# Turned attention tiles issued from SP, and a head norm with VectorE transposes, in a streaming-encoder layer

## The chip, the core and the metric

The kernel runs on one core of a Trainium2 chip. A core has TensorE (PE: matmuls, with PEld for the loading of its weights), VectorE (DVE), ScalarE (ACT), GpSimd (POOL) and SyncE (SP, which issues transfers); every engine works through its own list of instructions in order, and the engines wait for each other by semaphores. DMAs are issued from the queues of SP, ACT and POOL. The metric is the device time of one execution in microseconds (us).

## The reference

One layer of a streaming encoder, float32, sequence 512, model width 1024. A normed input goes through one input projection into four token mixers, whose outputs are each projected to 1024 channels, multiplied by a gate made of the same normed input, added up, and projected once more. Cross-attention into 256 memory tokens and a gated MLP follow. The change touches the mixers A and F and the preparation of the memory tokens:

```
# A: differential attention, 4 heads, two score maps each, chunk-causal mask
p = softmax(where(mask, s, -inf));  a = p[:, :, 0] - lam * p[:, :, 1]
o = einsum('bhqk,bkhe->bqhe', a, v)          # then a norm over each head's 128 channels
# F: forgetting attention, 8 heads, causal mask
s = q.k * scale + c[q] - c[k];  p = softmax(where(mask, s, -inf));  o = p.v
# norm of a head:  o * rsqrt(mean(o*o over 128 channels) + EPS) * gain
```

## The kernel before, in words

Products are made in three passes of float32r: every operand x is held as hi (x rounded by ScalarE, a copy) and lo (x minus hi, by VectorE), and each product is hi·hi, hi·lo, lo·hi into one PSUM bank of 512 columns. So each block of weights is loaded by SP into `wr` (L176, two buffers), cast by ACT into `wh` (L192) and its rest taken by DVE into `wl` (L193), four buffers each. A matmul helper (L235) and a PE transpose helper (L241) make nearly all of PE's work.

PSUM has eight banks in four pairs: `ps_mm` (projections), `ps_av` (in the attention stages the attention outputs; outside of them it alternates with `ps_mm`), `ps_sc` (scores), `ps_tr` (transposes).

The order of work. `run_blocks` goes through a list of weight blocks (the projections) and after each calls `bg.tick()`: a background planner that keeps a clock of estimated TensorE time (`bg.clock`, raised by each matmul and transpose), earns credit at 0.7 of it, and steps the background generators while they have credit. Each `yield cost, wait` of a generator tells what it has spent and how long it wants to stay away. The attention heads are such generators: `a_task(h)` for heads 0 to 3 of A, `f_task(p)` for pairs 0 to 3 of F. The framework's scheduler then fixes the order on every engine; `tc.issue_after(x)` keeps an instruction behind x there. `evacuations` holds the last ACT instruction that emptied a PSUM bank of a projection or a gate, `last_weights` the last weight cast.

One step of a head makes 128 rows of scores (`scores`, into `ps_sc`), adds mask or bias and takes the maximum (DVE, L929 in A, L1123 in F), exponentiates on ACT (L934, L1129), and scales by the reciprocal sum: in A by ACT (L938) and DVE (L939), in F for the pair's head j=1 by DVE (L1134) and for j=0 by ACT (L1136). In F POOL makes the bias `fbias` (L1117, L1119) from `ck`, the running sum of the log gates, which is spread over the partitions by a DMA from `crows`.

The values' product needs the probabilities transposed. Near heads (A's head 3, F's pairs 2 and 3) use PE transposes. Far heads (A's 0 to 2, F's 0 and 1) turn squares of 32x32 on DVE (L848), write the tile to DRAM (`put`, L853, queue of ACT) and read it back turned (`get`, L861, queue of POOL in A, of ACT in F), and split it in place (`split_in_place`: ACT cast L867, DVE rest L868). At the end of an A head its output is copied from `ps_av` (ACT, L948), transposed by four PE transposes, squared (ACT L954), summed (DVE L956), raised to -1/2 on POOL (`rstd_of`, L277 and L280), multiplied (DVE L958), transposed back by four PE transposes and split into `y8b` (ACT L158, DVE L159).

Mixers C and D come first, to about 208 us of the span; A's heads run beside projections and the gates of branch C to about 345; then come the values and forget gates of F (`vf_jobs`, `forget_gates`), F's pairs beside the gates and branch of A to about 535; then the gate of F's branch, during which `mem_task` turns the memory tokens (put on ACT, get on POOL, L1305), then cross-attention and MLP.

## Time and profile before

| what | value |
|---|---|
| median of 3 runs | 1052.34 us (1051.72 to 1052.66) |
| profiled execution, its own time | 1052.56 us |
| its span | 1050.8 us |
| PE busy | 1039.2 us, 99% of the span |
| DVE busy | 807.2 us, 77% |
| ACT busy | 508.9 us, 48% |
| POOL busy | 157.7 us, 15% |
| granted TensorE clock | 0.998 |

The span runs from the first to the last instruction of the profiled execution; its own time has 1.8 us more around it. Busy shares are means over stages. PE's matmuls overlap in the records, so the pace of PE is read from the starts of neighbouring matmuls and not from the duration of one: the record of a 512-column matmul says 0.39 us, but the next one starts 0.23 us later.

### The profile page before, as it was taken

To read this page: it belongs to the slowest core of one execution; us is meant where nothing else is said; L and a number is where in the kernel's file an instruction comes from. 1 tells how busy PE (TensorE), PEld (TensorE's weight loads), DVE (VectorE), ACT (ScalarE), POOL (GpSimd) and SP (SyncE) were. 2 spreads that over 40 slices of the span, in tenths; PEclk is the share of its full clock that TensorE was granted. 3 is DMA by queue.
4 is the path that set the end of the run, shared out by engine and by line. 5 is a ranking of instruction groups with operands and counts; after the bars stand their busy time and mean duration, and the time that the engine had idled before them with its cause. 6 is when DMAs were issued, how large, how long until landed. Compare 5 with 4: busy or idle time off the path is not lost.

```text
span 1050.8 us, 14439 instructions
## 1 busy us (share of the span) xinstructions
PE 1039.2 (99%) x5255; PEld 883.0 (84%) x5255; DVE 807.2 (77%) x1265; ACT 508.9 (48%) x838; POOL 157.7 (15%) x253
## 2 busy tenths in 40 slices
PE   9999999999999999999999999999999999999997
PEld 8888888888888988788888899999888888888886
DVE  7899998687777458776577898776767777667796
ACT  5322222376566355665434665655343333445662
POOL 4001000101210114422111031121112111111001
PEclk9999999999999999999999999999999999999999
DMA  7954333324433245652346834235676666725672
GB/s 249 316 164 104 103 99 100 101 83 124 134 104 111 60 120 172 182 149 82 100 154 230 277 121 124 78 101 182 194 246 221 220 223 219 220 81 181 214 216 80
DMA packets 175708, 163.85 MB, mean 156 GB/s; under 512 B 12543, under 2 KB 146924, under 8 KB 175637
## 3 DMA queue, kind: packets, MB, share of 16 engines
q1 hardware_dynamic: 152995, 119.91, 38.0%
q10 hardware_dynamic: 19122, 31.47, 8.9%
q0 software_dynamic: 3520, 11.56, 3.7%
q8 instruction: 41, 0.67, 0.3%
q14 instruction: 30, 0.25, 0.1%
HBM read 139.43 MB, written 23.48 MB: 155 GB/s over the span
## 4 chain that ended last, share of the span: by engine, by line
PE 90%; issue 4%; DVE 2%; ACT 1%; DMA 1%; POOL 1%; ACTq 0%; POOLq 0%; DVEq 0%
PE ps_mm L235 47%; PE ps_av L235 29%; PE ps_sc L235 7%; PE ps_tr L235 4%; PE ps_tr L241 2%; DMA ptl<-turned 1%; PE ps_mm L453 1%; PE ps_av L453 1%; POOL fbias L1117 0%; DMA xs<-in_x 0%; DVE qk L808 0%; ACT wh L192 0%; ACTq L861 0%; DVE e L1123 0%; DVE wl L193 0%
## 5 line engine op out<-in xcount | busy, mean ns | idle before, releaser
L192 ACT CAST wh<-wr 128x1024 fp32r<-128x1024 f32 (+1 forms) x140 | 146.7, 1048 | 258.9 <-PE ps_mm L235 156.9
L193 DVE TENSOR_TENSOR wl<-wr,wh 128x1024 fp32r<-128x1024 f32 (+1 forms) x140 | 174.2, 1245 | 86.3 <-ACT wh L192 86.0
L235 PE MATMUL ps_mm<-hth,wh 128*128 128x512 f32 (+1 forms) x616 | 230.8, 381 | 1.0 <-ACT wh L192 0.7
L235 PE MATMUL ps_mm<-hth,wl 128*128 128x512 f32 (+1 forms) x616 | 229.9, 379 | 0.0
L235 PE MATMUL ps_mm<-htl,wh 128*128 128x512 f32 (+1 forms) x616 | 229.8, 379 | 0.0
L235 PEld LDWEIGHTS ps_mm<-hth,wh 128*128 128x128 f32 x616 | 114.2, 188 | 22.5 <-ACT wh L192 1.1
L235 PEld LDWEIGHTS ps_mm<-hth,wl 128*128 128x128 f32 x616 | 114.0, 188 | 21.5
L235 PEld LDWEIGHTS ps_mm<-htl,wh 128*128 128x128 f32 x616 | 114.1, 188 | 20.4
L235 PE MATMUL ps_av<-htl,wh 128*128 128x512 f32 (+1 forms) x328 | 122.6, 374 | 0.0
L235 PE MATMUL ps_av<-hth,wh 128*128 128x512 f32 (+1 forms) x328 | 122.5, 373 | 0.0
L235 PE MATMUL ps_av<-hth,wl 128*128 128x512 f32 (+1 forms) x328 | 122.4, 373 | 0.0
L688 DVE SCALAR_TENSOR_TENSOR y<-y,par,y 128x508 f32<-128x508 f32 (+29 forms) x120 | 82.5, 726 | 0.1
L235 PEld LDWEIGHTS ps_av<-hth,wl 128*128 128x128 f32 x328 | 61.7, 188 | 10.9
L235 PEld LDWEIGHTS ps_av<-hth,wh 128*128 128x128 f32 x328 | 61.6, 188 | 10.9
L235 PEld LDWEIGHTS ps_av<-htl,wh 128*128 128x128 f32 x328 | 61.6, 188 | 10.8
L1683 DVE TENSOR_TENSOR wl<-dw,wh 128x1024 fp32r<-128x1024 f32 x32 | 40.0, 1256 | 15.5 <-ACT wh L1682 15.3
L1682 ACT CAST wh<-dw 128x1024 fp32r<-128x1024 f32 x32 | 33.4, 1051 | 22.6 <-PE ps_tr L235 8.1
L1117 POOL TENSOR_SCALAR fbias<-ck,cq 128x128 f32<-128x128 f32 (+3 forms) x32 | 28.3, 887 | 71.9 <-DVE st L1123 66.5
L1630 ACT ACTIVATE th<-c 128x512 f32<-128x512 f32 x22 | 13.9, 632 | 48.3 <-DVE c L615 48.3
L615 DVE SCALAR_TENSOR_TENSOR c<-ps_mm,par,c 128x510 f32<-128x510 f32 (+1 forms) x44 | 32.7, 744 | 0.7
L235 PE MATMUL ps_mm<-y8b,wh 128*128 128x512 f32 x96 | 30.6, 396 | 0.3 <-ACT ge L1165 0.3
L615 DVE SCALAR_TENSOR_TENSOR c<-ps_av,par,c 128x510 f32<-128x510 f32 (+1 forms) x40 | 29.8, 745 | 0.6
(486 smaller groups left out, 2103.5 us busy)
## 6 DMA issues: line engine op xcount, KB each, us to landing
wr<-in_w_up SPq DMA_DIRECT2D x44, 512.0 KB
wr<-in_w_in SPq DMA_DIRECT2D x38, 512.0 KB
wr<-in_w_gate SPq DMA_DIRECT2D x32, 512.0 KB
wp<-in_w_down ACTq DMA_DIRECT2D x22, 512.0 KB
sums<-wp ACTq DMA_DIRECT2D x22, 512.0 KB
dw<-sums SPq DMA_DIRECT2D x44, 256.0 KB
wr<-in_w_branch SPq DMA_DIRECT2D x16, 512.0 KB
wide<-in_w_out SPq DMA_DIRECT2D x12, 512.0 KB
```

The costliest lines, as they stand in the source:

```text
L192: last_weights[:] = [order(A.copy(hi, raw[:, :n])).ins, low.tensor_tensor(lo, raw[:, :n], hi.bitcast(F32), ALU.subtract).ins]
L193: low.tensor_tensor(lo, raw[:, :n], hi.bitcast(F32), ALU.subtract).ins]
L235: steps_of[:] = [PE.matmul(ps, lhs, rhs, start=start, stop=stop).ins]
L241: turns.append(PE.transpose(ps, x, ident[:n, :n]).ins)
L453: keep(PE.matmul(banks[c][:, :S // 2], w[p == 1][:, k, c * P:(c + 1) * P], ht[p == 2][:, i * 4 + k, :S // 2], start=(i, p, k) == (0, 0, 0) ...
L615: ins = V.scalar_tensor_tensor(dst[:, s:], src[:, :S - s], w(k), dst[:, s:], ALU.mult, ALU.add)
L688: ins = V.scalar_tensor_tensor(dst[:, s:], src[:, :S - s], pc("conv_dw", k * 4 + j), dst[:, s:], ALU.mult, ALU.add)
L1117: G.tensor_scalar(bias[:, :w], ck[j][:, :w], -1.0, cq[:, qt, head:head + 1], ALU.mult, ALU.add)
L1630: A.activation(th, c[:, 0], AF.Silu)
L1682: A.copy(hi, x)
L1683: V.tensor_tensor(lo, x, hi.bitcast(F32), ALU.subtract)
```

## The change

Four things are changed together.

- Transfers of turned tiles: `put` and `get` of the far heads, and both transfers of `mem_task`, are issued by SP. `get` isn't kept behind `evacuations` any more.
- The in-place split of A's far heads puts its ACT cast behind the last weight cast (`last_weights`) instead of the last evacuation.
- In F's far pairs the scaling of j=0 is done by DVE like that of j=1.
- The norm of A's heads: the output tile is turned by DVE in squares of 32x32 within SBUF, squared by ACT from SBUF, summed over the 32 columns of each square row (128x16), completed over the four partition groups by `over_channels` (one PE matmul of 16 columns into a `ps_tr` bank, L872), EPS is added by DVE, POOL raises 128x16 values to -1/2, DVE multiplies and turns back, and the split reads SBUF. The eight PE transposes of each head and one of its two `ps_tr` banks go.

```diff
     def put(e, w):
...
-        A.dma_start(d, e[:, :, :w])
+        SP.dma_start(d, e[:, :, :w])
         return d
...
-    def get(d, n, pt, local, queue=A):
-        with tc.issue_after(evacuations[0]) if queue is A else ExitStack():
-            queue.dma_start(part_of(pt[1], n, local).bitcast(F32), d.rearrange("(a j) (b x) -> (j b) a x", j=32, b=4))
-
-    def split_in_place(n, pt, local):
+    def get(d, n, pt, local):
+        SP.dma_start(part_of(pt[1], n, local).bitcast(F32), d.rearrange("(a j) (b x) -> (j b) a x", j=32, b=4))
+
+    def split_in_place(n, pt, local, after=evacuations):
         hi, lo = (part_of(x, n, local) for x in pt)
         raw = lo.bitcast(F32)
-        with tc.issue_after(evacuations[0]):
+        with tc.issue_after(after[0]):
             A.copy(hi, raw)
         V.tensor_tensor(lo, raw, hi.bitcast(F32), ALU.subtract)
...
-                    split_in_place(qt + 1, pt, qt % 2)
+                    split_in_place(qt + 1, pt, qt % 2, last_weights)
...
-                    get(es.pop(qt)[:, 0], qt + 1, pt, qt % 2, G)
+                    get(es.pop(qt)[:, 0], qt + 1, pt, qt % 2)
...
+        V.transpose(e[:, 1], e[:, 0])
+        A.activation(e[:, 0], e[:, 1], AF.Square, scale=1.0 / math.sqrt(P))
+        ms = m1p.tile([P, S // 32], F32, tag="ms4", name="ms4")
+        V.tensor_reduce(ms, by_token(e[:, 0]), AX.X, ALU.add)
+        yield 2.0, 4.0
         ps = bank("tr")
-        for t in range(NT):
-            transpose(ps[:, t * P:(t + 1) * P], e[:, 0, t * P:(t + 1) * P])
-        A.activation(e[:, 1], ps, AF.Square, scale=1.0 / math.sqrt(P))
-        ms = m1p.tile([P, NT], F32, tag="ms4", name="ms4", bufs=2)
-        V.tensor_reduce(ms, e[:, 1].rearrange("p (t c) -> p t c", t=NT), AX.X, ALU.add)
-        r = rstd_of(m1p, [ms], NT)
-        V.tensor_tensor(e[:, 0].rearrange("p (t c) -> p t c", t=NT),
-                        ps.rearrange("p (t c) -> p t c", t=NT),
-                        r.unsqueeze(2).to_broadcast([P, NT, P]), ALU.mult)
-        yield 1.5, 3.5
-        ps2 = bank("tr")
-        for t in range(NT):
-            transpose(ps2[:, t * P:(t + 1) * P], e[:, 0, t * P:(t + 1) * P])
+        over_channels(ps[:, :S // 32], ms)
+        V.tensor_scalar(ms, ps[:, :S // 32], EPS, None, ALU.add)
+        G.tensor_tensor(ms, ms, nhalf[:, :1].to_broadcast([P, S // 32]), ALU.pow)
+        yield 0.2, 4.0
+        V.tensor_tensor(by_token(e[:, 1]), by_token(e[:, 1]), ms.unsqueeze(2).to_broadcast([P, S // 32, 32]), ALU.mult)
+        V.transpose(e[:, 0], e[:, 1])
         if "a" not in y:
             y["a"] = (y8b(), y8b())
-        split(ps2, y["a"][0][:, h], y["a"][1][:, h], half["dn"])
-        yield 0.6, 0.0
+        split(e[:, 0], y["a"][0][:, h], y["a"][1][:, h], half["dn"])
+        yield 2.4, 0.0
...
-                    if j:
+                    if j or far:
                         V.tensor_scalar(e[:, j, :w], e[:, j, :w], st[:, 6 + j:7 + j], None, ALU.mult)
...
-            A.dma_start(d.rearrange("(p x) -> p x", p=P), m_t)
-            G.dma_start(y_t.rearrange("p (a x) -> p a x", a=4), d.rearrange("(a j b x) -> (j b) a x", a=4, j=32, b=4))
+            SP.dma_start(d.rearrange("(p x) -> p x", p=P), m_t)
+            SP.dma_start(y_t.rearrange("p (a x) -> p a x", a=4), d.rearrange("(a j b x) -> (j b) a x", a=4, j=32, b=4))
```

The changed estimates of cost in the `yield` lines shift where the planner places the heads' steps, so the order of matmuls on PE differs from the A stage to the end of the F stage. On PE 32 transposes of 128 columns go and 4 matmuls of 16 columns come; SP gets 52 transfers that ACT (20 puts, 16 gets, 2 of the memory) and POOL (12 gets, 2 of the memory) issued.

## Prediction

> **What bounds the kernel now.** I read the page's head first, then the waits of each engine between 200 and 535 us (the stages that the change reaches), then the timeline around each wait of PE.

> ```profile
> span 1050.8 us, 14439 instructions
> PE 1039.2 (99%) x5255; PEld 883.0 (84%) x5255; DVE 807.2 (77%) x1265; ACT 508.9 (48%) x838; POOL 157.7 (15%) x253
> PE ps_sc L235 <- DVE st L1123: 0.8, 1, 0.8
> PE ps_mm L235 <- ACT wh L192: 0.7, 1, 0.7
> PE ps_mm L235 <- ACT ge L1165: 0.3, 1, 0.3
> PE ps_mm L235 <- DVE qk L808: 0.2, 1, 0.2
> PE ps_tr L241 <- ACT e L948: 0.2, 1, 0.2
> 208.00:345.00 137.00, 136.77 (x682) 115.79 (x681) 103.38 (x230) 84.27 (x168) 16.79 (x26) 1.00 0.39 114
> 430.00:535.00 105.00, 104.28 (x528) 88.22 (x529) 69.28 (x145) 57.30 (x118) 26.88 (x41) 1.00 0.39 113
> ```

> PE is the bound, in the touched stages too (136.77 of 137 us; the columns are the stretch, its length and the busy us of PE, PEld, DVE, ACT and POOL). All idle time of PE between 200 and 535 us is in five waits. So a change here counts in two ways: by the matmuls that PE no longer has to issue, and by the few places where PE waits. Work of DVE, ACT, POOL and the queues costs nothing until it makes such a place.

> **PE's own work: -2.9 us.**

> ```profile
> 345.14 1.03 PE L241 MATMUL ps_tr<-ident,e 128*128 128x128 f32 x8
> 345.93 0.36 PE L235 MATMUL ps_mm<-wl,hth 128*128 128x256 f32 x1
> 346.13 0.28 PE L235 MATMUL ps_mm<-wh,htl 128*128 128x256 f32 x1
> 346.25 0.29 PE L235 MATMUL ps_mm<-wh,hth 128*128 128x256 f32 x1
> 186.10 0.29 PE L872 MATMUL ps_tr<-bn,across 128*128 128x16 f32 x2
> 186.24 0.48 PE L235 MATMUL ps_mm<-y8b,wh 128*128 128x512 f32 x1
> 186.55 0.39 PE L235 MATMUL ps_mm<-y8b,wl 128*128 128x512 f32 x1
> 186.78 0.62 PE L235 MATMUL ps_mm<-y8b,wh 128*128 128x512 f32 x2
> ```

> Eight transposes start at 345.14 and the next matmul at 345.93: 0.099 us each. The matmul behind them takes 0.20 to the next start where the one after takes 0.12: 0.08 lost per run of transposes. Thirty-two of them in up to eight runs cost 3.16 to 3.8 us; I take 3.5. A matmul with 16 columns (two records) takes 0.14, and the matmul behind it 0.31 in place of 0.23, so four cost 0.56 to 0.88; I take 0.6. Net -2.9 (bounds -2.3 and -3.2).

> **Waits that go: -3.0 us.**

> ```profile
> 427.56 0.62 PE L235 MATMUL ps_sc<-qk 128*128 128x512 f32 x2
> 429.03 0.73 PE L235 MATMUL ps_sc<-qk 128*128 128x512 f32 x2 [0.85 <-DVE st L1123]
> 430.42 0.47 PE L235 MATMUL ps_mm<-hth,wh 128*128 128x512 f32 x1 [0.66 <-ACT wh L192]
> 427.36 1.17 DVE L848 STREAM_TRANSPOSE e<-e 128x256 f32<-128x256 f32 x2 [0.90 <-DMA turned<-e]
> 437.82 2.35 ACTq L861 DMA_DIRECT2D ptl<-turned  x4
> 440.22 0.72 ACT L1136 ACTIVATE e<-e,st 128x512 f32<-128x512 f32 x1 [2.98 <-issue]
> 440.72 0.56 PE L235 MATMUL ps_sc<-qk 128*128 128x128 f32 x4
> 441.57 0.73 PE L235 MATMUL ps_mm<-y8b,wh 128*128 128x512 f32 x2 [0.30 <-ACT ge L1165]
> 350.11 0.62 PE L241 MATMUL ps_tr<-ident,e 128*128 128x128 f32 x4
> 350.94 0.66 PE L241 MATMUL ps_tr<-ident,e 128*128 128x128 f32 x4 [0.22 <-ACT e L948]
> ```

> By starts: two 512-column scores need 0.46, so 427.56 to 429.03 lost 1.0 and 429.03 to 430.42 lost 0.9. DVE came late there because its turn (L848) waited for a put that ACT had issued, with the scores' eviction (L1123) queued behind it. Four 128-column scores need 0.4, so 440.72 to 441.57 lost 0.4; ACT had first issued four gets (2.35 us), and the gate's Tanh (L1165) stood behind the delayed scaling. With put and get on SP neither queue holds compute, and one of the two scalings leaves ACT. 350.11 to 350.94 lost 0.4 in a transpose that is removed. With 0.2 to 0.3 at another place that the new order loosens, 3.0 go; the wait for L808 near 220 us, ahead of all edits, stays. Bounds: nothing goes but the 0.4 of the removed transpose, or all 3.0.

> **Waits that come: +3.6 us.** They follow from the new order of instructions, with durations from these rows:

> ```profile
> L818 DVE TENSOR_TENSOR qk<-ps_mm,qk 64x512 fp32r<-64x512 f32 x16 | 11.0, 688 | 3.5 <-ACT qk L816 3.4
> L929 DVE CUSTOM_DVE_ANT_0 e<-ps_sc,mask_a 128x384 f32<-128x384 f32 x8 | 4.2, 549 | 0.3 <-PE ps_sc L235 0.2
> L948 ACT COPY e<-ps_av 128x512 f32<-128x512 f32 x4 | 2.3, 581 | 3.5 <-PE ps_av L235 3.4
> L868 DVE TENSOR_TENSOR ptl<-ptl,pth 128x256 fp32r<-128x256 f32 x7 | 2.9, 423 | 1.2 <-ACT pth L867 1.2
> ACT pth L867 <- DMA ptl<-turned: 12.5, 7, 4.5
> ```

> - Near 264 us a projection block wants the `ps_mm` bank which two L818 subtractions empty, and these now stand behind a score eviction (L929) that PE itself feeds 1.25 us of matmuls earlier: 0.55 + 2 x 0.69 - 1.25, about 0.7, and 0.1 for the read of the maximum. 0.8 (0 to 1.4, both subtractions).
> - At the ends of heads 2 and 3 (about 344 and 348 us) the copy L948 out of `ps_av` is followed, in place of four transposes, by matmuls of `vf_jobs` into that bank: 0.44 us of other work before the first, none before the second. The row above with 0.44 us of cover lost 0.4; without cover it is 0.8. Sum 1.2 (0.4 to 1.6).
> - Head 2's last gets are issued when the value product of the first half has freed `ptl`, 6 us of matmuls ahead of use, and must land and be cast in that time. ACT's seven waits for such a tile were 1.8 us in the mean (the L867 row); I take 0.2, since most of one is covered (0 to 1.8).
> - The F stage begins with scores whose bias waits for the chain of forget gates; in the new order fewer matmuls lie beside it. What PE wants behind them is again a bank that two subtractions of 0.69 empty: 0.5 (0 to 1.4).
> - Near 404 us a gate product on DVE (L1177) stands behind in-place splits of F's pair 0, and these wait for gets: two or three L868 between, 0.9 (0 to 1.7, four).

> **Work that stays hidden.**

> ```profile
> L727 DVE STREAM_TRANSPOSE xn<-y 128x512 f32<-128x512 f32 x4 | 2.7, 697 | 0.0
> L722 POOL TENSOR_TENSOR bn<-bn,nhalf 128x16 f32<-128x16 f32 x1 | 2.9, 2930 | 96.2 <-DVE bn L705 96.2
> L1134 DVE TENSOR_SCALAR e<-e,st 128x512 f32<-128x512 f32 x4 | 1.9, 487 | 0.1
> SPq L176 <- DVE wl L193: 202.4, 33, 21.5
> ```

> A head's norm puts two square transposes (1.4 us) and a small addition more on DVE, about 1.5 us, and the power on POOL, 128x16 like the row of L722, takes 2.9. Nothing on PE waits for it but the 16-column matmul, which the planner places a step later, and `y8b` is needed only by the branch in the F stage. The far scaling puts eight operations on DVE, of 0.49 at the largest width: under 3.9 us over some 60. DVE idles 33 and 36 us in the two stretches shown, so both lie beside PE as long as they don't stand ahead of an eviction; where they do is in the list above. POOL loses 12 gets, whose waits for their puts stood ahead of its memsets and biases, ACT 16 gets and 20 puts. SP takes them: it waits 202 us of these 335 for a free `wr`, because the weights are loaded far ahead, so a weight load behind a get that waits for its put is late against nothing at once. If that cover is gone, each costs PE what the put takes. In the memory stage (from 535 us) two transfers move in the same way: nothing.

> **The sum.** -2.9 - 3.0 + 3.6 = -2.3 against the profiled execution's 1052.56, so 1050.3; that run lies 0.2 above the median of the three, so 1050.0 as a median. All good ends together (-3.2 - 3.0 + 0.4) give 1046.5; all bad ones (-2.3 - 0.4 + 7.9) 1057.5.

> **Rivals.**

> - No measurable change, about 1051.7: the waits come nearer to their upper ends (+5.3) and take back what PE saves. For it: the evictions in the list are on DVE, the second busiest engine. Against: PE's saving doesn't depend on them.
> - Slower, about 1056: SP's single queue. A get is issued only once its put has landed, and the next weight load stands behind it. In the F stage with its two pairs of far heads, loads that follow each other closely then reach ACT late, and PE waits for `wh`. A row shows that the margin isn't everywhere large:

> ```profile
> 365.93 1.05 ACT L192 CAST wh<-wr 128x1024 fp32r<-128x1024 f32 x1 [0.86 <-DMA wr<-in_w_in]
> ```

>   It decides once a hold is longer than a load's margin by more than the `wh` buffers cover. Four steps of gets in the F stage at 1.5 us each are 6: 1050 + 6. Against it: the 202 us of waiting above, and that this wait reached no matmul: none of PE's five waits lies there.
> - Larger gain, about 1047.5: with ACT and POOL free of transfers the evictions come earlier, and of the 3.6 us only the two copies (1.2) are left.
> - Slower by POOL's longer power, about 1056: if POOL and DVE exclude each other, a power of 2.9 us holds up DVE's evictions with two operands four times, 1.6 us each beyond PE's cover of 1.25: 6.5. This row speaks against it:

> ```profile
> 196.97 1.23 DVE L193 TENSOR_TENSOR wl<-wr,wh 128x1024 fp32r<-128x1024 f32 x1 [3.90 <-ACT wh L192]
> 199.69 1.23 DVE L193 TENSOR_TENSOR wl<-wr,wh 128x1024 fp32r<-128x1024 f32 x1 [0.82 <-ACT wh L192]
> 199.02 2.93 POOL L722 TENSOR_TENSOR bn<-bn,nhalf 128x16 f32<-128x16 f32 x1 [96.18 <-DVE bn L705]
> ```

>   That subtraction ran wholly inside the power's 2.93 us and took 1.23, no longer than the one before it, which ran ahead of the power. [...]

> **How the numbers follow.** Differences within 0.2% (2.1 us) can't be told from none. Chances: the forecast, 1049 to 1051.2 in itself, 0.45 (0.33 of it faster by over 0.2%, for the point lies on the edge of it); larger gain 0.15, faster; no change 0.20 (0.05 of it beyond +0.2%); SP's queue 0.14 and POOL's power 0.04, slower; the rest 0.02, slower. So faster 0.48, same 0.27, slower 0.25. The range 1047.0 to 1055.0 leaves out most of the two slow rivals and the best ends.

> **What would show it.** Right: PE has 32 records L241 fewer, no wait of ACT `wh` or DVE at 427 to 441 us, waits for the copy out of `ps_av` around 344 and 348, and SP's gets between weight loads without an ACT wait for `wr`. Wrong: ACT `wh` waits for `wr` and PE for `wh` in the F stage (SP's queue); DVE subtractions longer than 1.3 us while POOL is at the power; or several waits of PE for L929, L1123 or L818 of over 1 us.

## The result, and the profile after

The changed kernel takes 1054.53 us in the median of 15 runs (1053.10 to 1057.24), the kernel before 1052.14 us in 15 runs beside them. The ratio is 1.0022, 95% interval 1.0015 to 1.0029: slower by 2.4 us, where 2.1 us faster or a little more had been forecast. The profiled execution of the changed kernel took 1054.62 us with a span of 1052.8, 2.0 us more than the span before.

The head of the profile's page, and all waits of PE after between 200 and 640 us (engine and line that waited, what for, us in total, times, longest). Line numbers behind L860 are one to three lower than before: L1123 is now the negated maximum, which was L1126, and the score eviction, L1123 before, is now L1120.

```profile
span 1052.8 us, 14418 instructions
PE 1037.7 (99%) x5231; PEld 881.8 (84%) x5231; DVE 817.1 (78%) x1285; ACT 504.2 (48%) x830; POOL 155.2 (15%) x235
...
PE ps_mm L235 <- DVE v L156: 1.9, 1, 1.9
PE ps_mm L235 <- ACT ge L1162: 1.7, 1, 1.7
PE ps_av L235 <- ACT e L947: 0.7, 2, 0.5
PE ps_mm L235 <- DVE qk L818: 0.7, 1, 0.7
PE ps_mm L235 <- DVE qk L808: 0.2, 1, 0.2
```

PE is busy 1.5 us less, and its last matmul starts 1.65 us later: it waits more. The two waits near 428 us, for the score eviction and for `wh`, are gone, as forecast. Two large ones are new: 1.9 us for the values' rest (DVE v L156), at a place that the prediction did not list, and 1.7 us for the gate's Tanh (ACT ge), where 0.3 was to go to nothing.

How much of the 2.0 us belongs to the touched stages is read from the first matmul of cross-attention, in the timeline of before and of after:

```profile
640.53 0.28 PE L235 MATMUL ps_sc<-kxh,xqh 128*128 128x256 f32 x1
```

```profile
642.15 0.28 PE L235 MATMUL ps_sc<-kxh,xqh 128*128 128x256 f32 x1
```

1.6 us there. From here to the issue of the last output transfer nothing changes (1047.76 us before, 1049.41 after, 1.65 later). The remaining 0.4 of the span lies behind that issue, where PE has no work left; the profile gives no cause for it.

**The first new wait: 365 us, the end of F's values.** ACT, DVE and PE of the changed kernel:

```profile
364.61 1.05 ACT L192 CAST wh<-wr 128x1024 fp32r<-128x1024 f32 x1 [3.86 <-DMA wr<-in_w_in]
365.56 0.36 ACT L155 CAST v<-ps_mm 128x256 fp32r<-128x256 f32 x1
365.69 1.23 DVE L193 TENSOR_TENSOR wl<-wr,wh 128x1024 fp32r<-128x1024 f32 x1 [2.33 <-ACT wh L192]
366.83 0.42 DVE L156 TENSOR_TENSOR v<-ps_mm,v 128x256 fp32r<-128x256 f32 x1
365.17 0.28 PE L235 MATMUL ps_av<-wh,htl 128*128 128x264 f32 x1
367.31 0.50 PE L235 MATMUL ps_mm<-hth,wh 128*128 128x512 f32 x1 [1.85 <-DVE v L156]
```

And the same place on ACT and DVE before (the cast at 365.93 is in the prediction):

```profile
364.69 0.37 ACT L155 CAST v<-ps_mm 128x256 fp32r<-128x256 f32 x1 [2.89 <-PE ps_mm L235]
365.10 0.43 DVE L156 TENSOR_TENSOR v<-ps_mm,v 128x256 fp32r<-128x256 f32 x1 [2.01 <-ACT v L155]
```

In both kernels a weight load lands at about 365 us, and a weight cast waits for it. Before, the cast of the values (L155), which empties the `ps_mm` bank that PE wants next, stood ahead of that cast on ACT. After, it stands behind: it waits for a DMA that it has nothing to do with, and its rest on DVE stands behind the weights' rest (L193). The load itself is not later (364.6 after, 365.9 before).

**The second: 440 us, the gate beside F's pair 1.** DVE, ACT and PE after:

```profile
435.68 1.62 DVE L848 STREAM_TRANSPOSE e<-e 128x384 f32<-128x384 f32 x2
437.23 0.12 DVE L1123 TENSOR_SCALAR st<-st 128x2 f32<-128x2 f32 x1
437.39 0.58 ACT L1144 COPY e<-ps_av 64x512 f32<-64x512 f32 x1 [3.52 <-DVE st L1123]
437.88 0.72 ACT L1126 ACTIVATE e<-e,st 128x512 f32<-128x512 f32 x1
438.59 0.71 ACT L1126 ACTIVATE e<-e,st 128x512 f32<-128x512 f32 x1
439.30 0.57 ACT L1144 COPY e<-ps_av 64x512 f32<-64x512 f32 x1
439.77 1.04 ACT L192 CAST wh<-wr 128x1024 fp32r<-128x1024 f32 x1
440.84 0.69 ACT L1162 ACTIVATE ge<-ps_mm,s_b_gate 128x512 f32<-128x512 f32 x1
439.36 0.56 PE L235 MATMUL ps_sc<-qk 128*128 128x128 f32 x4
441.58 0.82 PE L235 MATMUL ps_mm<-y8b,wh 128*128 128x512 f32 x2 [1.66 <-ACT ge L1162]
442.20 0.63 PE L235 MATMUL ps_mm<-y8b,wl 128*128 128x512 f32 x1
442.63 1.05 PE L235 MATMUL ps_mm<-y8b,wh 128*128 128x512 f32 x2
```

ACT holds no gets any more and idles 3.5 us, but the Tanh stands behind two exponentials, two copies out of `ps_av` and a weight cast, and the exponentials need DVE's negated maximum (L1123). The matmuls that the Tanh reads ended at 436.75 us, four us before it ran. PE's four short scores (439.36) need 0.4 us, so by starts it loses 1.8 us. Behind the pause the matmuls come 0.43 us apart (442.20 to 442.63) and not 0.23; the windows show the granted clock (the number behind the five engines):

```profile
440.00:444.00 4.00, 2.42 (x7) 1.90 (x8) 3.94 (x7) 3.02 (x7) 0.00 (x0) 0.76 0.28 94
444.00:448.00 4.00, 4.00 (x16) 3.24 (x15) 4.00 (x10) 1.05 (x1) 0.37 (x1) 0.81 0.71 257
```

In the next four us it is 1.00 again. The same twelve matmuls took 2.84 us before (441.57 to 444.41) and take 4.44 here (441.58 to 446.02): 1.6 us more. Below, "the slow clock" means such a stretch.

### The profile page after: what moved, and what is told of

Its sections match the earlier page's. It is cut to its first block, busy times and chain, and to the rows that moved or that the text cites. A ratio compares the mean times of both kernels' runs of the same rounds, so it can differ in the third digit from the quotient of the medians.

```text
span 1052.8 us, 14418 instructions
## 1 busy us (share of the span) xinstructions
PE 1037.7 (99%) x5231; PEld 881.8 (84%) x5231; DVE 817.1 (78%) x1285; ACT 504.2 (48%) x830; POOL 155.2 (15%) x235
## 4 chain that ended last, share of the span: by engine, by line
PE 93%; DVE 2%; ACT 2%; issue 1%; DMA 1%; POOL 0%; POOLq 0%; DVEq 0%; SPq 0%; ACTq 0%
PE ps_mm L235 50%; PE ps_av L235 30%; PE ps_sc L235 7%; PE ps_tr L235 4%; PE ps_tr L241 2%; PE ps_mm L453 1%; PE ps_av L453 1%; ACT wh L192 1%; DVE wl L193 0%; DMA xs<-in_x 0%; DMA wr<-in_w_in 0%; DVE ptl L867 0%; DVE e L848 0%; ACT e L1126 0%; DVE e L1120 0%
## 5 line engine op out<-in xcount | busy, mean ns | idle before, releaser
L192 ACT CAST wh<-wr 128x1024 fp32r<-128x1024 f32 (+1 forms) x140 | 146.6, 1048 | 261.8 <-PE ps_mm L235 157.9
L193 DVE TENSOR_TENSOR wl<-wr,wh 128x1024 fp32r<-128x1024 f32 (+1 forms) x140 | 175.7, 1256 | 84.9 <-ACT wh L192 83.8
L235 PE MATMUL ps_mm<-hth,wh 128*128 128x512 f32 (+1 forms) x616 | 230.2, 380 | 2.1 <-DVE v L156 1.9
L235 PE MATMUL ps_mm<-htl,wh 128*128 128x512 f32 (+1 forms) x616 | 229.7, 379 | 0.0
L235 PE MATMUL ps_mm<-hth,wl 128*128 128x512 f32 (+1 forms) x616 | 229.4, 379 | 0.0
L235 PEld LDWEIGHTS ps_mm<-hth,wh 128*128 128x128 f32 x616 | 114.0, 188 | 23.5 <-DVE v L156 2.1
L235 PEld LDWEIGHTS ps_mm<-hth,wl 128*128 128x128 f32 x616 | 114.0, 188 | 21.7
L235 PEld LDWEIGHTS ps_mm<-htl,wh 128*128 128x128 f32 x616 | 114.0, 188 | 20.5
L235 PE MATMUL ps_av<-htl,wh 128*128 128x512 f32 (+1 forms) x328 | 122.5, 373 | 0.0
L235 PE MATMUL ps_av<-hth,wh 128*128 128x512 f32 (+1 forms) x328 | 122.4, 373 | 0.0
L235 PE MATMUL ps_av<-hth,wl 128*128 128x512 f32 (+1 forms) x328 | 122.3, 373 | 0.0
L235 PEld LDWEIGHTS ps_av<-hth,wl 128*128 128x128 f32 x328 | 61.6, 188 | 11.0
L235 PEld LDWEIGHTS ps_av<-hth,wh 128*128 128x128 f32 x328 | 61.6, 188 | 10.9
L235 PEld LDWEIGHTS ps_av<-htl,wh 128*128 128x128 f32 x328 | 61.6, 188 | 10.7
L235 PE MATMUL ps_mm<-y8b,wh 128*128 128x512 f32 x96 | 31.9, 410 | 1.7 <-ACT ge L1162 1.7
L235 PE MATMUL ps_mm<-y,wh 128*128 128x512 f32 x96 | 30.6, 395 | 0.7 <-DVE qk L818 0.7
```

The source lines that it names most:

```text
L192: last_weights[:] = [order(A.copy(hi, raw[:, :n])).ins, low.tensor_tensor(lo, raw[:, :n], hi.bitcast(F32), ALU.subtract).ins]
L193: low.tensor_tensor(lo, raw[:, :n], hi.bitcast(F32), ALU.subtract).ins]
L235: steps_of[:] = [PE.matmul(ps, lhs, rhs, start=start, stop=stop).ins]
```

## The experiments

All times are medians; "before" is the kernel before, run beside each experiment on the same chip. The ratios are to it. Times of two experiments can stem from different chips.

**Each part undone by itself.** First, put and get back on ACT and POOL, and with them the transfers of `mem_task` and the gets' place behind `evacuations` in F:

```diff
-        SP.dma_start(d, e[:, :, :w])
+        A.dma_start(d, e[:, :, :w])
...
-                    get(es.pop(qt)[:, 0], qt + 1, pt, qt % 2)
+                    get(es.pop(qt)[:, 0], qt + 1, pt, qt % 2, G)
```

> Changed kernel with put and get back on ACT and POOL; the other three parts stay. Theory (order of evictions): of the changed kernel's losses, the wait of PE for the gate's Tanh at 441.6 us (1.8 us, and 1.5 us of slow clock behind it) goes, because ACT has the Tanh ahead of the copies and the weight cast again; the wait at 367.3 us (2.0 us, DVE v L156) stays, because the third weight cast still stands ahead of the values' casts. Time about 1051.5, clock not below that of the kernel before. Rival (SP's single queue makes the weight load at 364.6 late): the wait at 367.3 us goes too, time about 1049.5.

1051.82 us (before 1051.98; ratio 0.9999, 0.9990 to 1.0008). Its ACT at the gate, and its longest wait of PE:

```profile
435.49 2.04 ACTq L861 DMA_DIRECT2D ptl<-turned  x4
438.19 0.72 ACT L1127 ACTIVATE e<-e,st 128x512 f32<-128x512 f32 x1 [4.79 <-issue]
439.62 0.67 ACT L1163 ACTIVATE ge<-ps_mm,s_b_gate 128x512 f32<-128x512 f32 x1
440.19 1.03 ACT L192 CAST wh<-wr 128x1024 fp32r<-128x1024 f32 x1
441.25 1.07 ACT L1145 COPY e<-ps_av 64x512 f32<-64x512 f32 x2
```

```profile
PE ps_mm L235 <- DVE v L156: 1.5, 1, 1.5
```

ACT idles 4.8 us ahead of the exponentials, with four gets and a put in its queue, and they start 1.5 us ahead of PE's short scores (439.65), as in the changed kernel. Yet PE loses only 0.3 us at the gate (its next matmul starts at 440.34), because the Tanh stands directly behind the exponentials, ahead of cast and copies. The wait at 367 us stays. So the moved transfers come with 2.7 us, and at the gate not by their queue but by the order that the scheduler chose once ACT had no gets. SP's queue as the cause of the wait at 367 us falls.

Second, the old norm:

```diff
-        V.transpose(e[:, 1], e[:, 0])
-        A.activation(e[:, 0], e[:, 1], AF.Square, scale=1.0 / math.sqrt(P))
...
+        ps = bank("tr")
+        for t in range(NT):
+            transpose(ps[:, t * P:(t + 1) * P], e[:, 0, t * P:(t + 1) * P])
```

> Changed kernel with the old norm (PE transposes). Theory: PE has 2.9 us more to do, the waits of 0.4 and 0.7 us at the heads' ends go, and the waits at 367.3 us (2.0) and 441.6 us (1.8 and the slow clock) stay, since both orders are as in the changed kernel: about 1056. Rival (the new norm itself costs the time, by its chain on DVE and POOL): about 1052, as before.

1056.53 us (before 1051.98; 1.0047, 1.0034 to 1.0060). That is 2.0 us above the changed kernel and near the theory. Both large waits stand as there (1.9 for DVE v, 1.7 for ACT ge), and a new one of 1.0 us for the gate product on DVE comes at 287 us, so this run by itself doesn't price the norm; the run with the norm and the values first, below, does. The place of the weight cast at 365 us is not the norm's alone: the other three parts lead to the same order here. Which of them does is not separated.

Third, the scaling of j=0 back on ACT:

```diff
-                    if j or far:
+                    if j:
```

> Changed kernel with the scaling of j=0 of the far pairs back on ACT; the order of matmuls is that of the changed kernel. Theory: DVE reaches the negated maximum (L1123) 0.4 us earlier, but ACT then scales ahead of the copies (0.6), and the Tanh still stands behind the exponentials, the copies and the weight cast: the wait at 441.6 us stays at 1.5 to 2.2 us and the time at 1054 to 1055. Rival (DVE's 3 us of added scaling cause that wait): it falls under 0.6 us, time about 1051.5.

1053.60 us (before 1051.98; 1.0015, 1.0006 to 1.0023). PE loses 0.9 us at the gate, between the two expectations: about half of the 1.8 us goes with DVE's added scaling, for the exponentials now start 3.05 us ahead of the short scores and not 1.5; the other half stays, with the Tanh still behind the copies and the cast. In its profile the slow clock follows the wait at 367 us:

```profile
368.00:372.00 4.00, 4.00 (x12) 3.19 (x11) 3.21 (x11) 1.74 (x3) 0.00 (x0) 0.58 0.48 140
```

Fourth, A's far casts behind the last evacuation again:

```diff
-                    split_in_place(qt + 1, pt, qt % 2, last_weights)
+                    split_in_place(qt + 1, pt, qt % 2)
```

> Changed kernel with the far heads' casts of A behind the last evacuation again. Theory: both orders at 367 and 441 us are unchanged, the place of these casts bears on 235 to 330 us alone, where the changed kernel loses 0.9 us at 262: the same time within 1 us, 1053.5 to 1055. Rival (the casts behind weights delay the evictions and cause the wait of 0.9 us at 262): 0.9 us less, and no wait at 262.

1052.28 us (before 1051.98; 1.0006, 0.9997 to 1.0014): 2.2 us less than the changed kernel. The rival was right about the wait at 262 us, and the time fell by more than its 0.9. ACT near 258 us, first in the changed kernel, then here:

```profile
258.23 0.51 ACT L866 CAST pth<-ptl 128x384 fp32r<-128x384 f32 x1
260.54 0.58 ACT L816 CAST qk<-ps_mm 64x512 fp32r<-64x512 f32 x1
```

```profile
260.25 0.58 ACT L816 CAST qk<-ps_mm 64x512 fp32r<-64x512 f32 x1
260.73 0.51 ACT L866 CAST pth<-ptl 128x384 fp32r<-128x384 f32 x1
```

Ordered behind the weight cast only, L866 moves ahead of the four casts that empty a `ps_mm` bank; their subtractions on DVE (L818) then fall behind a score eviction, and PE waits 0.7 us (0.9 by starts) at 262 us. Here this wait is gone, the one at 366 us is 0.4 shorter, and no slow clock shows in the profile (1.6): together the profiles' difference of 2.9 us.

**Repairs in the changed kernel.** The weight cast behind the values, by one edge that orders the two on ACT (`weight_casts` and `value_casts` only keep the instructions):

```diff
-            A.copy(hi, ps)
+            value_casts[:] = [A.copy(hi, ps).ins]
...
-                split(ps[t, g][:, :256].rearrange("p (h c) -> p h c", h=4), dst[0][:, t, hs, 0], dst[0][:, t, hs, 1])
+                split(ps[t, g][:, :256].rearrange("p (h c) -> p h c", h=4), dst[0][:, t, hs, 0], dst[0][:, t, hs, 1]); (t, g) == (2, 0) and tc.add_manual_dep(weight_casts[-1], value_casts[0].name, mybir.DependencyInfo(mybir.DependencyClass.NoSync, mybir.DependencyReason.DATA), reason="values first")
```

> Changed kernel, with the third weight cast of the end of the F values kept behind the first cast of the last values on ACT, as the kernel before has it; nothing else is edited, though the scheduler places the F stage anew. Theory (the place of one cast makes the wait of 2.0 us at 367.3): that wait falls under 0.3 us, the one at 441.6 stays if the Tanh still stands behind the copies: 1052.5, and 1.5 lower in runs without the slow clock behind it. Rival (the weight load is late and would hold PE there anyway): a wait of 1.5 to 2 us for wh or wl stands in the same place, time as the changed kernel.

1050.62 us (before 1052.04; 0.9985, 0.9976 to 0.9994). ACT there:

```profile
363.90 0.37 ACT L155 CAST v<-ps_mm 128x256 fp32r<-128x256 f32 x1 [2.92 <-PE ps_mm L235]
364.77 1.05 ACT L192 CAST wh<-wr 128x1024 fp32r<-128x1024 f32 x1 [0.50 <-DMA wr<-in_w_in]
```

One cast changes places, the wait of 2.0 us is gone, and the kernel is 3.9 us faster than the changed one. By the profiles 2.1 belong to the wait, 0.75 to the gate (1.1 by starts is left; the F stage is placed anew) and 1.6 to the slow clock, which doesn't show; the sum is a little more than the profiles' difference of 4.0. So about half of the 3.9 us is the one cast. The runs lie within 1.2 us of each other (1050.08 to 1051.32), those of the changed kernel within 4.1.

The turn behind the maximum:

```diff
-                V.tensor_scalar(st[:, 2:4], st[:, 0:2], -HD ** -0.5, None, ALU.mult)
-                turn_ready()
+                top = V.tensor_scalar(st[:, 2:4], st[:, 0:2], -HD ** -0.5, None, ALU.mult).ins
+                with tc.issue_after(top): turn_ready()
```

> Changed kernel, with the turn of an F pair's earlier tile (L848) kept behind the negated maximum (L1123) on DVE. Theory (ACT's exponentials start late because DVE does the turn first, and the Tanh stands behind them): the exponentials start 1.6 us earlier, the wait of 1.8 us at 441.6 falls to about 0.3, and with it the slow clock behind it in most runs: 1052.0 to 1053. Rival (the place of the Tanh behind copies and weight cast is enough by itself): a wait of over 1 us stays there, time about 1054.

1056.42 us (before 1052.04; 1.0036, 1.0024 to 1.0049): slower than the theory and the rival had it. DVE and ACT, and what PE waited for:

```profile
438.67 0.17 DVE L1123 TENSOR_SCALAR st<-st 128x2 f32<-128x2 f32 x1
439.22 1.63 DVE L848 STREAM_TRANSPOSE e<-e 128x384 f32<-128x384 f32 x2 [0.38 <-DMA turned<-e]
438.87 0.72 ACT L1126 ACTIVATE e<-e,st 128x512 f32<-128x512 f32 x1 [3.12 <-DVE st L1123]
440.93 1.07 ACT L1144 COPY e<-ps_av 64x512 f32<-64x512 f32 x2 [0.54 <-DVE st L1128]
442.97 0.69 ACT L1162 ACTIVATE ge<-ps_mm,s_b_gate 128x512 f32<-128x512 f32 x1
```

```profile
PE ps_mm L235 <- ACT ge L1162: 1.4, 1, 1.4
PE ps_mm L235 <- DVE ge L1174: 0.9, 1, 0.9
```

The turn does come after the maximum. Measured from PE's short scores, which start at 441.78 here, the exponentials come 1.4 us earlier than in the changed kernel (2.9 us ahead and not 1.5), close to the theory's 1.6. The Tanh comes only 0.3 us earlier, because ACT then waits 0.5 us and does both copies and the cast first. So the rival was right about the wait: the Tanh's place keeps it over 1 us. A later turn now stands ahead of the gate product (0.9 us), and in the profile the slow clock follows the wait at 367 us (granted clock 0.61 from 368 to 372 us).

The copies behind the Tanh:

```diff
-            A.copy(e[0:HD, j], av[j][HD:P])
+            with tc.issue_after(evacuations[0]): A.copy(e[0:HD, j], av[j][HD:P])
```

> Changed kernel with the two copies out of the F pairs' output banks kept behind the last gate's Tanh on ACT. Theory (the Tanh's place on ACT sets the wait at 441.6): the two copies (0.6 each) come after it, the exponentials and the weight cast stay ahead, so of the 1.8 us about 0.7 is left, and the slow clock is rarer; the wait of 2.0 us at 367 stays: 1053 to 1053.5. Rival (the wait is that for the exponentials' input, whatever stands between): 1.5 us or more is left, 1054 to 1054.5.

1053.72 us (before 1051.92; 1.0014, 1.0005 to 1.0022). The wait falls to 0.6 (0.8 by starts, 0.7 expected):

```profile
439.49 1.03 ACT L192 CAST wh<-wr 128x1024 fp32r<-128x1024 f32 x1
440.42 0.68 ACT L1162 ACTIVATE ge<-ps_mm,s_b_gate 128x512 f32<-128x512 f32 x1
441.12 1.07 ACT L1144 COPY e<-ps_av 64x512 f32<-64x512 f32 x2
```

The time is above the expectation by 0.2. The runs fall into two groups, four at 1052.2 to 1052.6 and seven at 1053.4 to 1054.6. A slow clock behind the untouched wait at 367 us would make such groups, but it is not shown: the profile, of a run in the lower group, has none, and two of the upper seven have a granted clock of 0.999.

**The norm by itself, and sums of repairs.** The kernel before with the new norm alone:

> The kernel before with the new norm alone. Theory: PE does 2.9 us less; the waits at the heads' ends (0.4 and 0.7) and the one at the end of the F values (1.7 to 2.0) come with the norm, the one at 262 doesn't (it belongs to the casts), and the one at 441 is as small as with put and get back: about 1050.5. Rival (the norm brings DVE work that the F stage or the A stage can't hide): about 1052 or above.

1051.12 us (before 1052.04; 0.9995, 0.9986 to 1.0004). The wait at the end of the values comes with the norm alone (1.3 us), and so does one at the gate (1.2; 0.3 had been expected), so most of the saving is waited away. At that gate the Tanh stands directly behind the exponentials, but these start only at 437.8 us, behind a put and four gets on ACT (435.00 to 437.79 us), though the maximum was ready at 435.0: the transfers on ACT cost there too.

The same with the values first:

> The kernel before with the new norm and the third weight cast behind the first values' cast. Theory: the norm's saving without its largest wait: 1049 to 1050, of the waits only those at the heads' ends (1.1 in sum) are new, and the two near 428 us are as in the kernel before, whose order the F stage takes again. Rival (the wait moves on to the next bank): as with the norm alone.

1049.83 us (before 1052.04; 0.9979, 0.9970 to 0.9988), as forecast. Its order of casts at 365 us is that of the kernel before, so 2.2 us is what the norm saves when no weight cast stands ahead of the values.

The norm, the far scaling and the values first:

> The kernel before with the new norm, the far scaling on DVE, and the weight cast behind the first values' cast; put and get stay on ACT and POOL. Theory: as with the norm and the values first (1049.8), and DVE's 0.4 us more per step of the far pairs shows in the waits near 426 us, where the scores already wait for DVE (1.6 us in sum there): 1050.0 to 1050.6. Rival (ACT is what is late there, freeing it of the scaling helps): 1049.2 or below.

1049.33 us (before 1052.14; 0.9979, 0.9967 to 0.9990). The rival is nearer: with the scaling on DVE the waits near 426 us (1.6 by starts in the kernel with the norm and the values first) are gone. A gain in time over that kernel is not shown: the median is 0.5 us lower, and the two ratios are the same. Two of the twelve runs took 1053.2 and 1054.1 us at a granted clock of 0.997; their cause stays open.

The changed kernel without its third part and with the values first, and then with the copies behind the Tanh too:

> Changed kernel without its third part (A's far casts stay behind the last evacuation) and with the weight cast of the F values behind the first values' cast. Theory: the two repairs add up, for they lie 100 us apart: against the run with the values first alone (1050.6) the wait of 0.8 us at 262 goes, the one of 1.1 us at the gate's Tanh near 438 stays: 1049.7. Rival (the freed time is waited for later, in the F stage): 1050.6 as there.

1050.17 us (before 1052.14; 0.9979, 0.9970 to 0.9988): 0.45 below the run with the values first alone, not 0.9, because a wait of 0.5 us for a cast of turned tiles (ACT pth L866) comes near 426 us. About half of the freed time is waited for later.

> Changed kernel without its third part, with the weight cast of the F values behind the first values' cast, and with the copies behind the Tanh. Theory: the repairs add up: against the run with the first two (1050.2) the wait of 1.1 us near 437 falls to 0 to 0.3: 1049.3. Rival (another eviction on ACT or DVE takes its place): 1050.2 or above.

1049.18 us (before 1051.92; 0.9974, 0.9963 to 0.9984): the lowest median here, 2.7 us below the kernel before, though not clear of the kernel with the norm, the scaling and the values first. Of PE's waits in the touched stages these are left:

```profile
PE ps_av L235 <- ACT e L947: 0.7, 2, 0.5
PE ps_mm L235 <- DVE qk L818: 0.5, 1, 0.5
PE ps_mm L235 <- DVE qk L808: 0.2, 1, 0.2
```

## Why the prediction was wrong

The gain that was forecast failed in two terms: the wait at the gate, which was to go, grew to 1.9 us (3.5 with the slow clock behind it), and a wait of 2.1 us at 367 us was not in the list of those that come. PE's own saving agrees with the sum, and the listed waits that came have about the sizes that were forecast.

**PE's own work, -2.9: agrees with the sum.** L241 has 54 records between 200 and 535 us where it had 86. The 2.9 us aren't measured by themselves. The sum by starts: -2.9, waits that went -3.4 (2.0 near 428 us, 0.5 at 441, 0.4 at 350, 0.2 at 395, and 0.3 of slower first matmuls behind them: the one at 430.42 us is followed after 0.31 us, the next after 0.23), waits that came +7.8 (below), makes +1.5; the first matmul of cross-attention is 1.6 later.

**Waits that go: right near 428 us, wrong at the gate.** The step that failed is "the gate's Tanh (L1165) stood behind the delayed scaling. With put and get on SP neither queue holds compute". The queue did become free. But the prediction took the Tanh's neighbours on ACT from the old trace. In the new order five instructions stand ahead of it, and 0.4 us became 1.8, with 1.6 of slow clock behind it in the profile. Two runs show it: with put and get back the exponentials are as late, the Tanh is next, and PE loses 0.3 us; with only the copies moved behind the Tanh it loses 0.8.

**Waits that come: three places sized well, three that stayed out, one missed.** By starts, with 0.1 of slower first matmuls in each (the one at 367.31 us is followed after 0.33 us, the next after 0.23):

| place | predicted | measured |
|---|---|---|
| 262 us, `ps_mm` behind L818 | 0.8 | 0.9 |
| 345 and 350 us, copies L947 | 1.2 | 0.5 + 0.8 |
| head 2's last gets | 0.2 | none |
| start of F's scores | 0.5 | none |
| 404 us, gate product behind L867 | 0.9 | none in this kernel |
| 367 us, values behind a weight cast | not listed | 2.1 |
| 441 us, Tanh | to go | 1.9 |
| slow clock behind it | not listed | 1.6 |

The two copies are priced almost exactly by "0.44 us of cover lost 0.4; without cover it is 0.8". The largest failure is the missing row at 367 us: the new order was searched for banks behind DVE and behind gets, and not for evictions behind a weight cast that waits for its load, though the prediction quotes that very cast (365.93, 0.86 for `wr`) and counts it as harmless because "this wait reached no matmul". It reached none because the values' cast stood ahead of it. With the cast moved by one edge the wait of 2.1 us is gone.

**Rivals.** Rival two (SP's queue) named the right direction, not the mechanism: the load at 365 us is as early as before, ACT's one long wait for `wr` (3.9 us) is there with the transfers off SP too (3.5 us), and the wait at 367 us stays. "No measurable change" had the right kind of mechanism, evictions that come late, but the waits came to 7.8 where it had 5.3, and over two thirds of that at places outside the list. That 7.8 is near the 7.9 of all bad ends together is thus luck. POOL's power runs beside DVE without harm, as the trace of before said:

```profile
358.37 2.90 POOL L958 TENSOR_TENSOR ms<-ms,nhalf 128x16 f32<-128x16 f32 x1 [4.75 <-DVE ms L957]
359.00 1.23 DVE L193 TENSOR_TENSOR wl<-wr,wh 128x1024 fp32r<-128x1024 f32 x1 [0.78 <-ACT wh L192]
```

A subtraction with two SBUF operands takes 1.23 inside the power's 2.90, and 1.23 at 365.69 us where no power runs. An eviction out of PSUM takes 0.41 inside a power (L156 at 351.84 us, the power from 350.72 to 353.62) and 0.42 outside of one (at 366.83).

**The range** ended at 1055.0 and held the median; the chance of 0.25 for slower was too small, since a net loss needed only one or two misplaced evictions.

## What to carry to other kernels

When one in-order engine is busy 99%, price an edit by the evictions that this engine waits for, and read their neighbours from the new order of instructions: an edit that frees a queue also moves what the scheduler puts into it, and one weight cast ahead of one bank's cast cost 2 us here. Keep an eviction from standing behind an instruction that waits for a DMA; one ordering edge repaired this. Measure the parts of a bundle by themselves and in pairs, for the far scaling cost 0.9 us at the gate in one order and removed 1.6 us of waits in another, and with put and get on ACT the wait at the gate was 0.3 us in one kernel and 1.2 in another.

## What the runs showed of the hardware

Pauses of 1.5 to 2.2 us in the profiles of five other kernels (put and get back, the old norm, A's casts back, the norm alone, the copies behind the Tanh) were followed by a clock of 1.00 in the windows behind them, and so was the pause at 367 us in the changed kernel itself. In the kernels without a pause over 1.2 us in the touched stages the clock was 1.00 from 364 to 376 and from 436 to 448 us. So the pause alone doesn't decide it; what does is not shown.

Such stretches fit the spread of one kernel's times: of the changed kernel's 15 runs six had a granted clock of 0.999 and took 1053.1 to 1053.7 us, the nine with 0.995 to 0.998 took 1053.7 to 1057.2. By these six the change costs about 1.1 us and not 2.4. In other kernels the mean clock sorts the runs less well, as with the copies behind the Tanh.
